# One more landing buffer for raw weight blocks, and new planner constants, in a two-layer encoder kernel

## The chip, the cores and the metric

The kernel runs on one core of one Trainium2 chip, as one program in one launch. The metric is device time in microseconds (us). Three runs of the kernel before gave 2086.12, 2087.95 and 2088.64 us; their median, 2087.95 us, is the time that the change is compared with. The profile and its trace are of one further execution of the same kernel.

## The reference

Two layers of an encoder work on 256 tokens of width 2048, all in float32. Cut to what the kernel's weight traffic is made of, a layer is:

```
h  = rms_norm(x, ln1_g);  proj = h @ w_in            # 2048 -> 4608
oa = neighborhood_attention(qa, ka, va, rpb)         # 8 heads, q and k normed with qn_a, kn_a
ob = windowed_gqa_sink(rope(qb), rope(kb), vb, sink) # 8 heads on 2, normed with qn_b, kn_b
x  = x + concat(rms_norm(oa), rms_norm(ob)) @ w_out  # 2048 -> 2048
u  = depthwise_conv(rms_norm(x, ln2_g) @ w_up)       # 2048 -> 2 x 5632, three taps and a bias
x  = x + (silu(u_gate) * u_up) @ w_down              # 5632 -> 2048
```

## The kernel before

**How a weight gets to TensorE.** All weights are read from HBM once, as half blocks of 128 x 1024 float32 (512 KB). A half block is loaded by the SP queue (`load`, L919 to L931) into a tile named `raw`, of which there are six. While the planner (below) is active, the room of the rope tables, `tabs`, serves as a seventh (L1202). TensorE multiplies in a rounded 32-bit format, so each weight is split into a high and a low part: ScalarE (ACT) copies the raw block into `whi` with rounding (`high_w`, L997), and VectorE (DVE) subtracts, `wlo = raw - whi` (`low_w_dve`, L1006). Every sixth `whi` lies in the room named `kT`. For some half blocks the low part is made by a transfer instead (`low_w`, L982 and L983): ACT writes the negated, rounded copy into `v_a` or `v_b`, and an accumulating DMA on the POOL queue adds the raw block to it. This text calls that copy the negated copy. When the last reader of a raw block is through, `free_raw` (L933) issues the next load into the same room, so a load waits, on the SP queue and in its order, until the block that was there before has been read. The activations are split in the same way (`xs`, `mid` and others hold high and low part), and three products (high x high, low x high, high x low) are summed in PSUM.

**The feed-forward half.** It takes about 630 us of each layer's 1040. An "up" quantum (two per group of 128 gate and 128 up columns) has two steps of eight matmul pairs each, a matmul of 512 columns with `whi` and one of 256 with `wlo`. `glu` then takes the result out of PSUM by two ACT copies (`read`, L646, tile `prob`), adds and scales them on DVE (L677, L649, tile `halo`), and runs the taps (L660, L662 on ACT, L687 on DVE, tile `pT`), SiLU (L689), the gating product (L666, tile `bias`) and its split (L670, L673). The down projection is done for most of the width by a scheme with seven products in place of eight: a "seven" quantum has three steps of six matmuls of 512 columns, into PSUM tiles `mm`, `tr`, `S` and `pv`. Its weight blocks come as two halves, and DVE makes sums of both halves for it: `sums_first` (L952, L953, into `prob_a`), which reads both raw halves, and `sums_second` (L958, L959, back into `raw`). Four sevens, one "plain" quantum and the "up" quanta between them make a group of some 64 us, and nine such groups follow each other in a layer. The seven holds one of two PSUM tiles named `mm`, so the "up" quantum behind it needs the other, and that one is free when both L646 copies of the "up" quantum before have run.

**What sets the order.** In this half the order on TensorE (PE), ACT, DVE and POOL is what the class `Plan` (L65 to L123) makes of a list of operations, each with an engine, a cost, a due time and dependences. `run` keeps a clock for each engine and always takes, of the operations that can begin first, the one that is due first. Due times of the weight work are set back from the step that needs it (`plan_weights`, L1014) by constants on L61: `AHEAD` for the negated copy, `HI` for `whi`, `LO` for `wlo`, `Z1` and `Z2` for the two sums. The planner keeps one clock for all transfers: L941 says that a raw half block holds it for 1.55 us and lands 2.0 us after that, L1040 says 2.9 and 2.3 us for an accumulating transfer. Each engine executes its list strictly in order, whatever the real times are. SP's order, and that of all other stages, is made by the scheduler of the language.

**Attention's room.** `add_square` (L187) sums the squares of attention's output: ACT writes a square into one of two tiles `sq` of 128 x 256, and POOL adds it to an accumulator (L191). `load_qk_g` (L297) loads the norm weights of q and k, 128 x 512, by a DMA; `rope_tables` (L311) and L314 read them on DVE. For layer 1 that load is issued when layer 0 has no more use for the room, at 231 us of the profiled execution.

Of the kernel before, what the change touches and what calls it, by code (L numbers as in the profile page):

```python
# [11 lines left out]
F32 = mybir.dt.float32  # L12
# [6 lines left out]
P = 128  # L19
L = 2  # L20
T = 256
# [3 lines left out]
HD = 128  # L25
# [32 lines left out]

EARLY = 6

AHEAD, HI, LO, Z1, Z2 = 9.0, 2.6, 1.0, 3.0, 2.0  # L61
STEP = {"up": 2.76, "seven": 1.365, "plain": 1.365, "": 1.365}


# [62 lines left out]
def encoder_kernel(  # L127
# [8 lines left out]
    act = ctx.enter_context(tc.tile_pool(name="act", bufs=1))  # L136
    work = ctx.enter_context(tc.tile_pool(name="work", bufs=2))
# [47 lines left out]
        return high  # L185

    def add_square(acc, src, first):  # L187
        sq = acc if first else work.tile([P, T], F32, name="sq", bufs=2)
        nc.scalar.activation(sq, src, AF.Square)
        if not first:  # L190
            nc.gpsimd.tensor_add(acc, acc, sq)  # L191
# [103 lines left out]
        rope["sin"], rope["cos"] = sin, cos  # L295

    def load_qk_g(l):  # L297
        par["qk_g"] = act.tile([P, 4, HD], F32, name="qk_g")
        nc.sync.dma_start(out=par["qk_g"], in_=a["qk_g"][l].partition_broadcast(P))

    def rope_tables(l):
# [330 lines left out]
    plan = Plan()  # L632
# [282 lines left out]
    raw, his, los, zs, loads, highs, homes = {}, {}, {}, {}, {}, {}, {}  # L915
# [3 lines left out]
    def load(parts=1, home="raw"):  # L919
        if loaded[0] < len(halves):  # L920
            q, h = k = halves[loaded[0]]
            loaded[0] += 1
            homes[k] = home
            if home == "raw":
                raw[k] = wp.tile([P, 1024], F32, name="raw", bufs=HALVES)
            else:
                raw[k] = act.tile([P, 1024], F32, name=home)
            m = 1024 // parts
            for j in range(parts):
                loads[q] = nc.sync.dma_start(out=raw[k][:, j * m:(j + 1) * m],  # L930
                                             in_=quanta[q][0][:, h * 1024 + j * m:h * 1024 + (j + 1) * m])  # L931

    def free_raw(k):  # L933
        del raw[k]
        home = homes.pop(k)
        if home == "raw" or plan.active:
            load(1, home)
            if plan.active and loaded[0] < len(halves):
                k2 = halves[loaded[0] - 1]
                plan.issued = max(plan.issued, plan.now, plan.done.get(("sent", *k), 0.0))  # L940
                plan.dma(("raw", *k2), plan.issued, 1.55, 2.0)  # L941

    kind_of = lambda s: quanta[steps[s][0]][2]
    is_seven = lambda s, part: s < len(steps) and kind_of(s) == "seven" and steps[s][1] == part
# [10 lines left out]
    def sums_second(q):  # L955

        z, u, w = pair(zs[q]), pair(raw[q, 0]), pair(raw[q, 1])
        nc.vector.tensor_add(u[:, 1], u[:, 1], z[:, 0])  # L958
        nc.vector.tensor_sub(u[:, 0], u[:, 1], w[:, 1])  # L959
        free_raw((q, 1))  # L960
# [7 lines left out]
    def by_transfer(s):  # L968
        q, half = steps[s]
        return half == 1 and (quanta[q][2] == "plain" or last_up.get(q, False))  # L970
# [22 lines left out]
    def high_w(s):  # L993

        if s < len(steps) and s not in his:
            his[s] = place(s, "whi")
            highs[s] = nc.scalar.activation(his[s], source(s), AF.Copy)  # L997
            if s in los:
                free_raw(steps[s])
# [14 lines left out]
    def plan_weights(s, slots):  # L1014

        q, part = steps[s]
        due = ideal[s]
        kind = kind_of(s)
        high, low = ("high_w", s), ("low_w", s)
        from_raw = [("raw", q, part)] if kind != "seven" else [("raw", q, 0)]  # L1020
        prev = [("high_w", s - 1)]
        here = lambda: (q, part if kind != "seven" else 0) in raw
        both = lambda: (q, 0) in raw and (q, 1) in raw
        slot = lambda: slots[-SPLIT_AHEAD - 1:-SPLIT_AHEAD]
        full = [("pe", *steps[s - SPLIT_AHEAD - 2])]
        if s in his and s in los:
            if not by_transfer(s):
                slots.append(("pe", q, part))
            return
        assert s not in his, s  # L1030
        if by_transfer(s):
            if s in los:
                plan.act(high, 1024, due - HI, lambda: high_w(s), prev + full, when=here)
                return
            n = turns[0] + len(sends)
            sends.append(("pe", q, part))

            def send():
                low_w(s)
                plan.dma(low, plan.now + 0.9, 2.9, 2.3)  # L1040
                plan.done["sent", q, part] = plan.done[low]

            plan.act(("negate", s), 1024, due - AHEAD, send, from_raw + sends[-3:-2] + ([("negate", negs[-1])] if negs else []), when=here)
            negs.append(s)
            plan.act(high, 1024, due - HI, lambda: high_w(s), [("negate", s)] + prev + full, when=here)
            return
        if kind == "seven" and part:
            need = [("z", q)] if part == 1 else [("z2", q)]
        else:
            need = from_raw  # L1050
        plan.act(high, 1024, due - HI, lambda: high_w(s), need + prev + full, when=here)
        plan.dve(low, 1024, due - LO, lambda: low_w_dve(s), [high] + order[-1:] + slot())
        order[:] = [low]
        slots.append(("pe", q, part))
        if kind == "seven" and part == 0:
            plan.dve(("z", q), 512, due - Z1, lambda: sums_first(q), from_raw + [("raw", q, 1)] + zlast, 2, when=both)
            zlast[:] = [("low_w", s + 1), ("z2", q)]
            plan.dve(("z2", q), 512, due - Z2, lambda: sums_second(q), [("z", q), high, low], 2)
# [59 lines left out]
    par = {}  # L1118
# [52 lines left out]
    first = {q for q in range(len(quanta)) if quanta[q][2] == "seven" and all(quanta[q - i][2] == "up" for i in range(1, 5))}  # L1171
    first = {q - 2 * (PART - 1) for q in first}
# [9 lines left out]
    def start_plan(s):  # L1182
        for e in plan.free:
            plan.free[e] = ideal[s]
        plan.active = True
        turns[1] = 0
        z = s
        while kind_of(z):
            z += 1
        for n in range(z, z + SPLIT_AHEAD):  # L1190
            assert kind_of(n) == ""
        slots = [("pe", *steps[i]) for i in range(s - SPLIT_AHEAD - 1, s) if not by_transfer(i)]
        sends[:], negs[:], order[:], zlast[:] = [], [], [], []
        for i in range(s, z + SPLIT_AHEAD):
            plan_weights(i, slots)
        for i in range(s, z):
            def body(i=i):
                q, part = steps[i]
                quanta[q][1](q, part, his.pop(i), los.pop(i))
            plan.op(("pe", *steps[i]), "PE", STEP[kind_of(i)], ideal[i], body,  # L1200
                    needs(i) + ([("pe", *steps[i - 1])] if i > s else []))
        load(1, "tabs")  # L1202

    for s, (q, half) in enumerate(steps):
        if s + SPLIT_AHEAD < KD // 2:
# [123 lines left out]
```

## Time and profile before

| | |
|---|---|
| median of three runs | 2087.95 us (2086.12 to 2088.64) |
| profiled execution, its own time | 2090.57 us |
| its span, first to last instruction | 2088.5 us |
| TensorE clock granted | 1.000 |
| busy share of the span | PE 99%, PEld 85%, DVE 82%, ACT 74%, POOL 8% |
| moved by DMA | 472.48 MB, mean 226 GB/s |

The profiled execution took 2.07 us more than its span, and 2.62 us more than the median of the runs. A row of the timeline reads: start, duration, engine, source line, operation, tiles written and read, shapes, count, and in brackets how long the engine had been idle before it and what ended that. A row of the waits reads: who waited for whom, us in total, times, longest. PE is TensorE's matmuls and PEld its weight loads; matmuls overlap, and the end of each is modelled.

### The profile page before, as it was taken

Reading aid. Unit: us, or ns where it says so; the run is one execution under the profiler, and the core shown is the slowest. Engines: PE = TensorE matmul, PEld = TensorE weight load, DVE = VectorE, ACT = ScalarE, POOL = GpSimd, SP = SyncE. Lnnn points to the kernel's source line nnn. Section 1 sums busy time; section 2 is a strip of 40 time slices with the busy share of each in tenths; the row PEclk is TensorE's granted clock in tenths of the full one; section 3 lists DMA queues with packets and bytes.
Section 4 is the critical chain, followed back from the end, with each engine's and each line's share of the span. In section 5 each row is a group of like instructions: output and inputs, shape, how many; then the busy total and the mean of one; then the engine's idle time right before and its main releaser. Section 6 shows DMA issues by size and latency. Waiting matters only on the chain.

```text
span 2088.5 us, 30567 instructions
## 1 busy us (share of the span) xinstructions
PE 2072.3 (99%) x10720; PEld 1767.6 (85%) x10720; DVE 1711.1 (82%) x2576; ACT 1548.8 (74%) x2595; POOL 157.3 (8%) x170
## 2 busy tenths in 40 slices
PE   9999999999999999999999999999999999999999
PEld 8888888888888888888888888888888888888887
DVE  7786655889999999999757766568899999999995
ACT  7566557987888888888555665579888888888883
POOL 0011100000000000000000111000000000000000
PEclk9999999999999999999999999999999999999999
DMA  9655557888888888888765555578788888888884
GB/s 347 202 164 168 166 179 213 243 236 231 259 250 247 262 248 250 246 254 256 231 182 175 171 168 167 176 214 241 239 247 242 257 256 262 248 241 259 253 250 148
DMA packets 134010, 472.48 MB, mean 226 GB/s; under 512 B 15329, under 2 KB 17889, under 8 KB 133857
## 3 DMA queue, kind: packets, MB, share of 16 engines
q1 hardware_dynamic: 117872, 413.87, 60.6%
q0 software_dynamic: 15264, 55.58, 14.3%
q8 instruction: 84, 1.38, 0.3%
q10 hardware_dynamic: 720, 1.08, 0.2%
q14 instruction: 70, 0.57, 0.1%
HBM read 412.80 MB, written 2.10 MB: 199 GB/s over the span
## 4 chain that ended last, share of the span: by engine, by line
PE 62%; DVE 18%; DMA 11%; issue 5%; ACT 4%; DVEq 0%; ACTq 0%; POOLq 0%; SPq 0%
PE mm L165 55%; DVE wlo L1006 8%; DMA raw<-in_w_up 5%; DMA raw<-in_w_seven 3%; PE S L165 2%; ACT whi L997 2%; PE pv L165 2%; DVE pT L687 1%; PE tr L165 1%; DMA tabs<-in_w_up 1%; DVE halo L649 1%; DVE prob L677 1%; DVE raw L958 1%; DVE x L800 1%; DVE x L805 1%
## 5 line engine op out<-in xcount | busy, mean ns | idle before, releaser
L165 PE MATMUL mm<-xs,whi 128*128 128x512 f32 x2320 | 813.2, 391 | 9.3 <-ACT prob L646 9.1
L1006 DVE TENSOR_TENSOR wlo<-raw,whi 128x1024 fp32r<-128x1024 f32 x535 | 651.5, 1220 | 187.1 <-ACT whi L997 161.9
L997 ACT ACTIVATE whi<-raw 128x1024 fp32r<-128x1024 f32 x613 | 640.1, 1054 | 212.6 <-PE mm L165 169.3
L165 PE MATMUL mm<-xs,wlo 128*128 128x256 f32 x2112 | 597.1, 283 | 0.0
L165 PEld LDWEIGHTS mm<-xs,whi 128*128 128x128 f32 x2320 | 435.2, 188 | 109.7 <-ACT prob L646 19.3
L165 PEld LDWEIGHTS mm<-xs,wlo 128*128 128x128 f32 x2112 | 398.9, 189 | 4.5 <-DVE wlo L1006 0.4
L165 PE MATMUL mm<-whi,xs 128*128 128x512 f32 x1152 | 294.8, 393 | 0.2 <-ACT whi L997 0.2
L165 PE MATMUL mm<-whi,mid 128*128 128x512 f32 x928 | 255.4, 393 | 0.4 <-ACT v_a L330 0.4
L165 PEld LDWEIGHTS mm<-whi,xs 128*128 128x128 f32 x1152 | 212.9, 188 | 42.8 <-ACT whi L997 0.6
L165 PEld LDWEIGHTS mm<-whi,mid 128*128 128x128 f32 x928 | 169.9, 188 | 34.1 <-ACT v_a L330 0.9
L165 PE MATMUL mm<-xs,kT 128*128 128x512 f32 x496 | 174.6, 390 | 0.0
L165 PE MATMUL mm<-wlo,xs 128*128 128x512 f32 x576 | 158.9, 392 | 0.0
L662 ACT ACTIVATE pT<-halo,conv 128x256 f32<-128x256 f32 x352 | 157.7, 496 | 0.0
L165 PE MATMUL mm<-wlo,mid 128*128 128x512 f32 x486 | 152.5, 393 | 0.0
L687 DVE TENSOR_TENSOR pT<-pT 128x512 f32<-128x512 f32 x176 | 121.0, 687 | 12.3 <-ACT pT L660 4.1
L165 PEld LDWEIGHTS mm<-wlo,xs 128*128 128x128 f32 x576 | 107.1, 188 | 21.4
L646 ACT ACTIVATE prob<-mm 128x512 f32<-128x512 f32 x176 | 102.4, 584 | 30.5 <-PE mm L165 29.5
L165 PEld LDWEIGHTS mm<-xs,kT 128*128 128x128 f32 x496 | 93.1, 188 | 19.5
L165 PEld LDWEIGHTS mm<-wlo,mid 128*128 128x128 f32 x486 | 90.9, 188 | 19.2
L660 ACT ACTIVATE pT<-halo,conv 128x256 f32<-128x256 f32 x176 | 103.4, 589 | 0.0
L165 PE MATMUL mm<-xs,v_a 128*128 128x256 f32 x352 | 99.3, 282 | 0.0
L165 PE MATMUL mm<-xs,v_b 128*128 128x256 f32 x352 | 99.3, 282 | 0.0
(233 smaller groups left out, 2958.4 us busy)
## 6 DMA issues: line engine op xcount, KB each, us to landing
raw<-in_w_up SPq DMA_DIRECT2D x302, 512.0 KB, 5.2
raw<-in_w_in SPq DMA_DIRECT2D x142, 512.0 KB, 4.4
raw<-in_w_seven SPq DMA_DIRECT2D x126, 512.0 KB, 5.3
raw<-in_w_out SPq DMA_DIRECT2D x64, 512.0 KB, 3.8
tabs<-in_w_up SPq DMA_DIRECT2D x50, 512.0 KB, 5.1
v_a<-raw POOLq DMA_DIRECT2D x46, 512.0 KB, 6.4
v_b<-raw POOLq DMA_DIRECT2D x46, 512.0 KB, 6.5
raw<-in_w_plain SPq DMA_DIRECT2D x32, 512.0 KB, 5.7
```

What stands on the lines that cost most here:

```text
L165: nc.tensor.matmul(ps, lhsT, rhs, start=start, stop=stop, skip_group_check=True)
L646: nc.scalar.activation(own[part], ps[:, :, part], AF.Copy)
L649: nc.vector.tensor_mul(ux[:, :, r:r + T], own[0], st["r2"][:, None, :].to_broadcast([P, 2, T]))
L660: nc.scalar.activation(own["y"][:, j], src, AF.Identity, scale=taps[j][i], bias=taps[j][3])
L662: nc.scalar.activation(own[name][:, j], src, AF.Copy, scale=taps[j][i])
L677: plan.dve(k("sum"), 512, e + 5.0, lambda: nc.vector.tensor_add(own[0], own[0], own[1]), [k("t"), k("t2")])
L687: lambda n=n: nc.vector.tensor_add(own["y"], own["y"], own[n]),
L800: plan.dve(k("x_2"), 1024, e + 13.4, lambda: add(x_2, x_2, both(ps[5])), [("pe", q, 2), k("x12b")])
L805: plan.dve(k("x2_"), 1024, e + 22.0, lambda: add(x2_, x2_, both(cur["t"])), [k("t7"), k("x_2"), k("x21")])
L958: nc.vector.tensor_add(u[:, 1], u[:, 1], z[:, 0])
L997: highs[s] = nc.scalar.activation(his[s], source(s), AF.Copy)
L1006: nc.vector.tensor_sub(los[s], source(s), his[s].bitcast(F32))
```

## The change

The change has two parts.

**Room.** The squares and the norm weights, until now two tiles of 128 x 256 and one of 128 x 512, become parts of one tile `aux` of 128 x 1024: `add_square` alternates between its third and fourth quarter, and the norm weights are its first half. While the planner is active, `aux` takes one more raw half block, as `tabs` does (`load(1, "aux")` in `start_plan`). So eight half blocks have room where seven had.

**Constants.** The planner's due times move ahead (`AHEAD` 9.0 to 10.5, `HI` 2.6 to 3.2, `LO` 1.0 to 1.4, `Z1` 3.0 to 4.2, `Z2` 2.0 to 3.5), and its transfers take longer: a raw half block 1.65 us on the transfer clock (was 1.55) and 3.2 us from there to its landing (was 2.0), an accumulating one 3.2 us to its landing (was 2.3).

```
-AHEAD, HI, LO, Z1, Z2 = 9.0, 2.6, 1.0, 3.0, 2.0
+AHEAD, HI, LO, Z1, Z2, TAKES, LANDS = 10.5, 3.2, 1.4, 4.2, 3.5, 1.65, 3.2
...
     def add_square(acc, src, first):
-        sq = acc if first else work.tile([P, T], F32, name="sq", bufs=2)
+        if first:
+            sq = acc
+        else:
+            par["square"] ^= 1
+            sq = par["aux"][:, 512 + T * par["square"]:512 + T * par["square"] + T]
...
     def load_qk_g(l):
-        par["qk_g"] = act.tile([P, 4, HD], F32, name="qk_g")
+        par["aux"], par["square"] = act.tile([P, 1024], F32, name="aux"), 0
+        par["qk_g"] = par["aux"][:, 0:4 * HD].rearrange("p (w d) -> p w d", w=4)
...
-                plan.dma(("raw", *k2), plan.issued, 1.55, 2.0)
+                plan.dma(("raw", *k2), plan.issued, TAKES, LANDS)
...
-                plan.dma(low, plan.now + 0.9, 2.9, 2.3)
+                plan.dma(low, plan.now + 0.9, 2.9, LANDS)
...
         load(1, "tabs")
+        load(1, "aux")
```

After the change the kernel's lines stand four lines lower from L192 on, and five from L300 on: L997 is L1002, L1006 is L1011, L982 is L987, L930 is L935, L646 is L651, L952 is L957.

**The loads on SP** in layer 0, for the "up" step whose negated copy ACT begins at 497.36 us of the profiled execution, two blocks ahead of it and the two around it. The names in brackets are what a load waits for: DVE, ACT or the landing of an earlier DMA (DMAHW an ordinary one, DMASW an accumulating one). Before, with that step's block going into `raw_4859`:

```order
L930 DMA raw_4816<-in_w_up 128x1024 [waits DMAHW0_49,DVE_49]
L930 DMA raw_4842<-in_w_up 128x1024 [waits DMAHW2_49,DVE_49]
L930 DMA tabs_4848<-in_w_up 128x1024 [waits DMAHW5_49,DMASW5_49,Activation_49]
L930 DMA raw_4859<-in_w_up 128x1024 [waits DMAHW3_49,DVE_49]
L930 DMA raw_4890<-in_w_seven 128x1024 [waits DMAHW4_49,DVE_49]
```

Now the same five blocks, the step's block going into `tabs_4836`:

```order
L935 DMA raw_4773<-in_w_up 128x1024 [waits DMAHW7_49,DMAHW0_49,DVE_49]
L935 DMA raw_4804<-in_w_up 128x1024 [waits DVE_49]
L935 DMA raw_4830<-in_w_up 128x1024 [waits DMAHW1_49,DVE_49]
L935 DMA tabs_4836<-in_w_up 128x1024 [waits DMAHW2_49,DMAHW4_49,DMASW5_49,Activation_49]
L935 DMA raw_4847<-in_w_seven 128x1024 [waits DMAHW3_49,DVE_49]
```

Each block now waits for the release that the block ahead of it waited for: the wait for ACT and an accumulating DMA stood at the third load and stands at the fourth, with that step's block.

**ACT** around the same negated copy (`v_a`), down to the two copies out of PSUM (`prob<-mm`) that TensorE needs. Before:

```order
L997 ACTIVATE whi<-prob_a 128x1024
L982 ACTIVATE v_a<-raw 128x1024
L689 ACTIVATE prob<-pT 128x256
L997 ACTIVATE whi<-raw 128x1024
L670 ACTIVATE mid<-bias 128x256
L997 ACTIVATE whi<-raw 128x1024 x2
L646 ACTIVATE prob<-mm 128x512
L997 ACTIVATE kT<-tabs 128x1024
L646 ACTIVATE prob<-mm 128x512
```

Now:

```order
L1002 ACTIVATE whi<-prob_a 128x1024
L694 ACTIVATE prob<-pT 128x256
L987 ACTIVATE v_a<-tabs 128x1024
L675 ACTIVATE mid<-bias 128x256
L1002 ACTIVATE whi<-raw 128x1024 x3
L651 ACTIVATE prob<-mm 128x512
L1002 ACTIVATE kT<-raw 128x1024
L651 ACTIVATE prob<-mm 128x512
```

SiLU (`prob<-pT`) moves ahead of the negated copy; the other copies keep their places but for one. In most later groups SiLU moves back instead, at 28 places in all: at half of them behind one `whi` copy, at the others behind the negated copy and one `whi` copy.

**DVE** a few us later at the same place, where the two sums of a seven's halves (`prob_a`) stand with the subtractions (`wlo`) and the sum of the "up" results (`prob<-prob`). Before:

```order
L1006 TENSOR_TENSOR wlo<-raw,whi 128x1024
L677 TENSOR_TENSOR prob<-prob 128x512
L1006 TENSOR_TENSOR wlo<-tabs,kT 128x1024
L649 TENSOR_TENSOR halo_115<-prob,acc_b 128x2x256
L952 TENSOR_TENSOR prob_a<-raw 128x512
L953 TENSOR_TENSOR prob_a<-raw 128x512
```

Now:

```order
L1011 TENSOR_TENSOR wlo<-raw,whi 128x1024
L957 TENSOR_TENSOR prob_a<-raw,aux 128x512
L958 TENSOR_TENSOR prob_a<-aux,raw 128x512
L682 TENSOR_TENSOR prob<-prob 128x512
L1011 TENSOR_TENSOR wlo<-raw,whi 128x1024
L654 TENSOR_TENSOR halo_115<-prob,acc_b 128x2x256
```

The two sums, which read both halves of a seven's block, have moved ahead of the addition and of one subtraction.

Two moves outside the planner: the first raw block that goes into `aux` is loaded during the output projection, behind attention's last square; and layer 1's norm weights are no longer loaded at 231 us but at the end of layer 0's feed-forward half, when the last weight block in `aux` has been split. There the first L316 of layer 1 stands on DVE right behind the subtraction that reads that last block, and waits for the load of the norm weights.

## The prediction

> **What bounds the kernel now.** I read the page first, then TensorE's waits, then the places where it waits.
>
> ```profile
> span 2088.5 us, 30567 instructions
> ## 1 busy us (share of the span) xinstructions
> PE 2072.3 (99%) x10720; PEld 1767.6 (85%) x10720; DVE 1711.1 (82%) x2576; ACT 1548.8 (74%) x2595; POOL 157.3 (8%) x170
> ```
>
> TensorE is busy for 99% of the span, and the change takes no matmul away. What can go is idle time. TensorE's waits say for whom:
>
> ```profile
> PE mm L165 <- ACT prob L646: 9.1, 17, 0.9
> ...
> PE pv L165 <- DVE wlo L1006: 0.8, 3, 0.3
> ...
> PE S L165 <- DVE wlo L1006: 0.2, 1, 0.2
> ```
>
> 17 waits are for the copy out of PSUM (L646), four for a low part. Idle time is less than what a wait costs, because the end of a matmul is modelled past the moment at which the next could start. The chain of waits gives the pace without waits, the timeline the start on either side of a wait:
>
> ```profile
> 420.66 1.36 PE S L165 x6
> ```
>
> ```profile
> 502.57 0.39 PE L165 MATMUL mm<-wlo,mid 128*128 128x512 f32 x1
> 503.84 0.50 PE L165 MATMUL mm<-xs,whi 128*128 128x512 f32 x1 [0.88 <-ACT prob L646]
> ```
>
> Six matmuls of 512 columns take 1.36 us, 0.227 each, while one is shown as 0.39. The one at 503.84 could have started at 502.57 + 0.23 = 502.80, so 1.04 us were lost, 0.88 shown and 0.16 hidden. The 17 waits cost 9.1 + 17 x 0.16 = 11.8 us, the four for low parts 1.0 + 4 x 0.16 = 1.6 us: together 13.4 us, 0.64% of the span. This is all that the change can win.
>
> Why ACT is late with L646 stands in its timeline:
>
> ```profile
> 497.36 1.06 ACT L982 ACTIVATE v_a<-raw 128x1024 fp32r<-128x1024 f32 x1 [2.73 <-DMA raw<-in_w_up]
> 498.32 0.40 ACT L689 ACTIVATE prob<-pT 128x256 f32<-128x256 f32 x1
> 498.63 1.05 ACT L997 ACTIVATE whi<-raw 128x1024 fp32r<-128x1024 f32 x1
> 499.58 0.40 ACT L670 ACTIVATE mid<-bias 128x256 fp32r<-128x256 f32 x1
> 499.89 2.00 ACT L997 ACTIVATE whi<-raw 128x1024 fp32r<-128x1024 f32 x2
> 501.79 0.57 ACT L646 ACTIVATE prob<-mm 128x512 f32<-128x512 f32 x1
> 502.26 1.05 ACT L997 ACTIVATE kT<-tabs 128x1024 fp32r<-128x1024 f32 x1
> 503.21 0.58 ACT L646 ACTIVATE prob<-mm 128x512 f32<-128x512 f32 x1
> ```
>
> ACT stood 2.73 us before the negated copy, because its raw block had not landed. Behind that it runs without a gap up to the second L646, which ends at 503.79; TensorE starts at 503.84. So of the 2.73 us of waiting 1.04 reach TensorE: the slack here is 1.69 us. These waits recur:
>
> ```profile
> ACT v_a L982 <- DMA raw<-in_w_up: 32.3, 18, 4.9
> ...
> ACT v_b L982 <- DMA raw<-in_w_up: 28.9, 16, 4.1
> ```
>
> 34 waits, 61.2 us, 1.8 us on average. The planner believed that the block would be there.
>
> **The change part by part.**
>
> *The eighth room.* The rows of the order show that every load gets the release that the load ahead of it had. What that does to the landing is read from the block and the one ahead of it:
>
> ```profile
> 489.39 0.33 SPq L930 DMA_DIRECT2D tabs<-in_w_up  x1
> 489.82 0.38 SPq L930 DMA_DIRECT2D raw<-in_w_up  x1
> ```
>
> ```profile
> tabs<-in_w_up SPq DMA_DIRECT2D x1, 512.0 KB, 6.6
> raw<-in_w_up SPq DMA_DIRECT2D x1, 512.0 KB, 7.5
> ```
>
> The block ahead landed at 489.39 + 6.6 = 496.0, this one at 489.82 + 7.5 = 497.3. If issues move up by one place in an unchanged stream of transfers, this block lands when the one ahead did, 1.3 us earlier. ACT's wait falls to 2.73 - 1.3 = 1.4 us, below the slack of 1.69: the 1.04 us are gone. I check the place with the longest wait of layer 1 that I found:
>
> ```profile
> 1859.37 1.06 ACT L982 ACTIVATE v_a<-raw 128x1024 fp32r<-128x1024 f32 x1 [2.85 <-DMA raw<-in_w_up]
> ```
>
> ```profile
> 1864.76 0.39 PE L165 MATMUL mm<-wlo,mid 128*128 128x512 f32 x1
> 1865.86 0.50 PE L165 MATMUL mm<-xs,whi 128*128 128x512 f32 x1 [0.70 <-ACT prob L646]
> ```
>
> ```profile
> 1851.24 0.33 SPq L930 DMA_DIRECT2D raw<-in_w_up  x1
> 1852.06 0.33 SPq L930 DMA_DIRECT2D raw<-in_w_up  x1
> ```
>
> ```profile
> 1852.06 7.23 DMA raw<-in_w_up
> ```
>
> ```profile
> raw<-in_w_up SPq DMA_DIRECT2D x1, 512.0 KB, 6.8
> ```
>
> The loss is 1865.86 - 1864.99 = 0.87 us, the slack 2.85 - 0.87 = 1.98. The block landed at 1859.29; the one ahead, whose row of the DMA view is the last, 6.8 us after 1851.24, at 1858.0. 1.3 us earlier leaves a wait of 1.6, again under the slack. The longest of the 17 idle times is 0.9, a loss of 1.04, and 1.3 is more than that. Taken at full, the eighth room wins the 11.8 us. I keep 0.9 of it, 10.6 us, for places where a second delay stands close behind the first.
>
> *Is there transfer time for it?* The windows around the place:
>
> ```profile
> 480.00:485.00 5.00, 5.00 (x28) 4.27 (x27) 4.96 (x8) 3.85 (x4) 0.86 (x1) 1.00 0.50 129
> 485.00:490.00 5.00, 4.71 (x23) 3.37 (x22) 5.00 (x8) 3.98 (x6) 0.00 (x0) 1.00 1.04 287
> 699.00:763.00 64.00, 63.66 (x341) 54.72 (x340) 60.22 (x86) 53.57 (x89) 4.36 (x5) 1.00 0.85 254
> ```
>
> The last two columns are the DMA engines' share and GB/s. Half of the five us before the burst is idle, 2.5 us; a half block at the 287 GB/s of the burst takes 524 KB / 287 = 1.8 us and fits.
>
> On how long such a block takes, a rule of the Trainium skill stands against this change. "DMA: Bandwidth & Descriptors", section "Anatomy of one DMA", fits a transfer from the POOL queue as 2.0 us plus its bytes over 436 GB/s; that makes an estimate of 3.2 us for 512 KB. By it the block of 489.82 would land at 493.0, ACT would never wait, and the eighth room would win nothing. The row shows 7.5 us, so the trace disagrees: blocks queue behind each other here.
>
> *The constants.* On ACT the same copies stand between the negated copy and the second L646; only SiLU (0.40 us) changes sides. Where it moves ahead, slack grows by 0.3; where it moves back, L646 sees the same instructions before it. Moving SiLU back, at 28 places of the order, delays the gating product on DVE by one or two copies of 0.95 us (499.58 - 498.63). What covers it is that the seven that reads the product comes only some steps later, by the planner's due times a dozen us. I cost it at nothing; without that cover it would be up to 28 x 1.4 = 40 us of DVE's waiting, which reaches TensorE only through late `wlo`. The larger `LO`, `Z1` and `Z2` put weight work earlier on DVE, which is what the four waits for low parts lack; I take half of their 1.6 us, 0.8.
>
> *The room's other users.* Squares alternate between two quarters as between two tiles: nothing. The norm weights of layer 1 add a wait on DVE at the layers' boundary: the first L316 waits for a landing, and behind it queue an addition to x and the next subtractions. The nearest rows:
>
> ```profile
> 1017.92 1.23 DVE L1006 TENSOR_TENSOR wlo<-raw,whi 128x1024 fp32r<-128x1024 f32 x1 [0.48 <-ACT whi L997]
> 1023.22 1.23 DVE L1006 TENSOR_TENSOR wlo<-raw,whi 128x1024 fp32r<-128x1024 f32 x1 [4.08 <-PE mm L165]
> ```
>
> ```profile
> bias<-in_bias SPq DMA_DIRECT2D x1, 160.0 KB, 3.8
> ```
>
> The subtraction that frees `aux` is the one at 1017.92 and ends at 1019.15. A small load then lands 3.8 us later, at 1023.0, inside the 4.08 us that DVE waits for TensorE anyway. So nothing is lost. If the landing takes the 7.5 us of a busy stretch instead, DVE is 3.5 us late, and at worst TensorE too; below nothing it can't go, as no wait ends there.
>
> *The sum*, against the profiled execution: span 2088.5 - 10.6 - 0.8 = 2077.1, its own time 2090.57 - 11.4 = 2079.2. That execution was 2.6 us above the median of the runs. From the median, 2087.95 - 11.4 = 2076.5 us.
>
> **The rivals.**
>
> *A landing follows its issue* (0.14). If each block keeps its 7.5 us from issue to landing, only the issue's 0.43 us (489.82 - 489.39) count: 0.43 of 1.04, 41% of 11.8 = 4.9 us, 2083.0 us. For it: the small load at the boundary landed after 3.8 us, these after 6.6 and 7.5; what stretches a landing in a busy stretch may stretch it whenever it was issued. Against it: 6.6 and 7.5 us for two blocks issued 0.43 us apart, a queue and not a fixed time.
>
> *The bound moves to DVE or nothing moves* (0.09). DVE is busy 60.2 of 64 us in a group. If it takes over each stall as ACT's lateness goes, or SP's loads are held by something that I don't see, the time stays within 4 us of 2088. Against it: without the losses (11.8 us over 18 groups, 0.7 each) a group takes 63.3 us, and DVE still has 3.1.
>
> *Slower: the sums wait in front of the others* (0.05).
>
> ```profile
> DVE prob_a L952 <- DMA raw<-in_w_seven: 23.6, 25, 2.5
> ```
>
> DVE already waits 25 times for a seven's second half. `Z1` puts the sums 1.2 us earlier, ahead of the addition and a subtraction, which now queue behind that wait, and L649 and TensorE behind these. At full, 25 x 1.2 = 30 us of new DVE waiting. If half reaches TensorE, 15 - 11.4 makes 2091.6 us. It decides from 11.4 of 30, 38%. Against it: these blocks too land 1.3 us earlier, which cancels the 1.2, and 3.1 us per group are spare.
>
> **How the numbers follow.** The forecast, losses nearly gone, has 0.72: 2076.5 us, between 2073 (13.4 us and a little more, 2087.95 - 13.4 = 2074.6, less a spread of about 1.3 between runs) and 2080 (the norm weights' 3.5 us lost). A landing that follows its issue reaches to 2083. The range 2073 to 2083 holds these two, 0.86. A measurement here can tell about 0.2%, 4.2 us, from no change. Faster by more than that, below 2083.8: 0.72 + 0.14 and a little of the third case, 0.87. Within it 0.09, slower 0.04.
>
> **What would show it.** In the profile after: PE's waits for the L651 copy fall from 17 and 9.1 us to a few and under 2; ACT's waits of the negated copy for DMA fall from 61 us to under 30, by about 1.3 us each; the load at this place is issued at the former one's moment and lands 1.3 us earlier against TensorE's steps; DVE waits under 4 us at the first L316 of layer 1 with no wait of TensorE behind it. I am wrong if ACT's waits shrink and TensorE's don't (something else is close behind), if landings keep 7.5 us from their issue, or if PE's waits for low parts (`wlo`) grow.

## The result, and the profile after

The kernel after takes 2070.26 us (median of 6 runs, 2069.91 to 2070.64), the kernel before 2088.3 us on the same chip (6 runs, 2086.12 to 2091.91): a ratio of 0.9911, 95% interval 0.9898 to 0.9924, 18.0 us less. The forecast was 2076.5 us, with a range from 2073 to 2083: the direction was right, and the gain larger than the range allowed, and larger than the 13.4 us that the prediction called all that could be won. The profiled execution after took 2070.64 us, with this span and busy time:

```profile
span 2068.9 us, 30510 instructions
...
PE 2062.4 (100%) x10720; PEld 1769.9 (86%) x10720; DVE 1706.1 (82%) x2576; ACT 1549.3 (75%) x2595; POOL 157.6 (8%) x170
```

The span is 19.6 us shorter. All of it is in the feed-forward halves, counted here from the first transposes of `x` (L216 before), which begin inside the output projection, so that they are longer than the stretch that the planner orders: layer 0's lasts 727.6 us where it lasted 737.5, layer 1's 735.4 where it lasted 745.2, and attention of layer 1 with both boundaries 302.9 us in both kernels.

TensorE's waits after, in us in total, times, longest:

```profile
PE pv L165 <- DVE halfpi L161: 1.1, 1, 1.1
PE mm L165 <- ACT whi L179: 0.7, 1, 0.7
PE mm L165 <- ACT v_a L335: 0.4, 2, 0.2
```

The 17 waits for the copy out of PSUM and the four for a low part in the feed-forward halves are gone from these rows; what is left stands in attention and at the start. At the place that the prediction worked out, SP's queue now shows the load of the step whose negated copy goes to `v_a`:

```profile
485.80 0.33 SPq L935 DMA_DIRECT2D tabs<-in_w_up  x1
```

ACT after it:

```profile
493.00 1.07 ACT L987 ACTIVATE v_a<-tabs 128x1024 fp32r<-128x1024 f32 x1 [0.30 <-DMA tabs<-in_w_up]
...
497.99 0.59 ACT L651 ACTIVATE prob<-mm 128x512 f32<-128x512 f32 x1
498.48 1.05 ACT L1002 ACTIVATE kT<-raw 128x1024 fp32r<-128x1024 f32 x1
499.43 0.59 ACT L651 ACTIVATE prob<-mm 128x512 f32<-128x512 f32 x1
```

And TensorE at the matmul that waits for the second of these two copies out of PSUM (before, the one at 503.84):

```profile
501.65 0.40 PE L165 MATMUL mm<-wlo,mid 128*128 128x512 f32 x1
501.88 0.39 PE L165 MATMUL mm<-xs,whi 128*128 128x512 f32 x1
502.12 0.28 PE L165 MATMUL mm<-xs,wlo 128*128 128x256 f32 x1
```

ACT's wait for the block is 0.30 us where it was 2.73, the second copy ends at 500.02, and TensorE's matmul comes 0.23 us after the one ahead of it, without a wait. The load is issued 501.88 - 485.80 = 16.1 us ahead of this matmul; before it was 502.80 - 489.82 = 13.0 us ahead of the moment at which the matmul could have run. So it is issued 3.1 us earlier against TensorE's work, not 0.43. It still takes 7.1 us to land.

A group of the feed-forward half, whose window took 64.00 us before:

```profile
697.00:760.30 63.30, 63.30 (x341) 54.90 (x340) 60.22 (x86) 54.25 (x89) 4.37 (x5) 1.00 0.85 255
```

It takes 63.30 us, with TensorE (the first number behind the window's length) busy in all of it and DVE (the third) for the same 60.22 us as before: DVE had those 3.1 us to spare and has not become the bound.

### The profile page after: what moved, and what is told of

It is laid out like the page before. It is cut to its first block, busy times and chain, and to the rows that moved or that the text cites. A ratio compares the mean times of both kernels' runs of the same rounds, so it can differ in the third digit from the quotient of the medians.

```text
span 2068.9 us, 30510 instructions
## 1 busy us (share of the span) xinstructions
PE 2062.4 (100%) x10720; PEld 1769.9 (86%) x10720; DVE 1706.1 (82%) x2576; ACT 1549.3 (75%) x2595; POOL 157.6 (8%) x170
## 3 DMA queue, kind: packets, MB, share of 16 engines
q1 hardware_dynamic: 117872, 413.87, 61.2%
## 4 chain that ended last, share of the span: by engine, by line
PE 99%; DMA 0%; ACT 0%; ACTq 0%; DVE 0%; issue 0%
PE mm L165 85%; PE S L165 6%; PE pv L165 4%; PE tr L165 3%; PE tr L460 1%; PE tr L381 1%; PE S L220 1%; DMA mid<-in_xT 0%; ACT v_a L335 0%; ACT whi L1002 0%; ACT mid L182 0%; ACT xs L182 0%; DVE x L872 0%; ACTq L1105 0%; ACTq L1098 0%
## 5 line engine op out<-in xcount | busy, mean ns | idle before, releaser
L1011 DVE TENSOR_TENSOR wlo<-raw,whi 128x1024 fp32r<-128x1024 f32 x503 | 613.0, 1220 | 185.0 <-ACT whi L1002 162.4
L1002 ACT ACTIVATE whi<-raw 128x1024 fp32r<-128x1024 f32 x569 | 596.2, 1055 | 222.2 <-PE mm L165 182.8
L667 ACT ACTIVATE pT<-halo,conv 128x256 f32<-128x256 f32 x352 | 157.8, 498 | 0.0
L651 ACT ACTIVATE prob<-mm 128x512 f32<-128x512 f32 x176 | 103.6, 591 | 50.2 <-PE mm L165 49.8
L665 ACT ACTIVATE pT<-halo,conv 128x256 f32<-128x256 f32 x176 | 103.7, 590 | 0.0
```

Source lines behind the costliest of these rows:

```text
L651: nc.scalar.activation(own[part], ps[:, :, part], AF.Copy)
L665: nc.scalar.activation(own["y"][:, j], src, AF.Identity, scale=taps[j][i], bias=taps[j][3])
L667: nc.scalar.activation(own[name][:, j], src, AF.Copy, scale=taps[j][i])
L1011: nc.vector.tensor_sub(los[s], source(s), his[s].bitcast(F32))
```

## A measure that closes the account

TensorE's rows of waits do not add up to 19.6 us, since they count only what is left after the modelled end of the matmul before. The weight loads (PEld) end sooner, so the same waits show more of themselves there. Before:

```profile
PEld mm L165 <- ACT prob L646: 19.3, 25, 1.3
PEld pv L165 <- DVE wlo L1006: 3.4, 7, 0.8
PEld S L165 <- DVE wlo L1006: 1.1, 3, 0.6
```

25 waits for the copy, not 17, and ten of the two kinds of waits for low parts that the prediction counted as four. One that the matmul's rows do not show at all stands at 552.49 (before, timeline of TensorE's two queues):

```profile
552.14 0.40 PE L165 MATMUL mm<-wlo,qtok 128*128 128x512 f32 x1
552.49 0.19 PEld L165 LDWEIGHTS mm<-xs,whi 128*128 128x128 f32 x1 [0.39 <-ACT prob L646]
552.49 0.50 PE L165 MATMUL mm<-xs,whi 128*128 128x512 f32 x1
552.79 0.19 PEld L165 LDWEIGHTS mm<-xs,wlo 128*128 128x128 f32 x1
552.82 0.36 PE L165 MATMUL mm<-xs,wlo 128*128 128x256 f32 x1
```

The matmul starts 0.35 us after the one ahead of it, 0.12 more than the 0.23 of the pace, and its row has no bracket. The next one starts 0.33 us later, another 0.10: its weights could not be loaded ahead. The same restart stands behind the long wait at 503.84:

```profile
503.84 0.50 PE L165 MATMUL mm<-xs,whi 128*128 128x512 f32 x1 [0.88 <-ACT prob L646]
504.18 0.28 PE L165 MATMUL mm<-xs,wlo 128*128 128x256 f32 x1
504.30 0.39 PE L165 MATMUL mm<-xs,whi 128*128 128x512 f32 x1
504.53 0.28 PE L165 MATMUL mm<-xs,wlo 128*128 128x256 f32 x1
```

0.34 us from the first to the second, and then 0.12 for 256 columns and 0.23 for 512.

So I count **late starts**: for each two consecutive matmuls of the two feed-forward halves, the time between their starts less the pace of the first (0.227 us for 512 columns, 0.118 for 256), where more than 0.06 us is left. Before this gives 98 late starts, 21.9 us: 26 of over 0.18 us, 14.6 us; 33 small ones right behind another late one, 3.5 us; 39 other small ones, 3.8 us. After it gives 27, 2.6 us. The difference, 19.3 us, is the span's 19.6. Of it 14.2 us are stalls, 3.4 us restarts behind them, and 1.7 us delays too small for a row.

The second measure, **lead**, puts each load, landing and negated copy on a clock that counts only TensorE's work (the paces of the matmuls begun by then), and compares it with the same load or copy of before: a mean over 444 loads and 84 copies inside the two feed-forward halves. After, landings come 3.4 us earlier than before, and negated copies 1.7 us earlier.

All kernels by these measures but e4, which is told below. The runs with e1 to e3, with e5 to e8 and with e9 to e12 were made on three other chips than the first, so kernels of different groups are best compared by their ratios. Rooms is the number of half blocks that have room; told is what the planner believes of landings; due the five due times. The ratio is to the kernel before on the same chip, with its 95% interval. The last column is what ACT waited for landings at the negated copies.

| kernel | rooms | told | due | us | ratio | span | late starts, us | landings earlier | copies earlier | ACT's waits |
|---|---|---|---|---|---|---|---|---|---|---|
| before | 7 | old | old | 2088.3 | | 2088.5 | 21.9 | 0 | 0 | 69.8 in 40 |
| room alone (e1) | 8 | old | old | 2086.80 | 0.9985 [0.9974, 0.9996] | 2083.6 | 16.8 | 2.3 | 1.6 | 70.1 in 42 |
| constants alone (e2) | 7 | new | new | 2080.36 | 0.9959 [0.9946, 0.9973] | 2077.4 | 10.4 | -1.0 | -1.2 | 18.9 in 10 |
| six rooms (e3) | 6 | old | old | 2109.22 | 1.0090 [1.0068, 1.0112] | 2107.2 | 40.9 | -3.1 | -2.7 | 92.0 in 68 |
| e5 | 8 | new | old | 2070.83 | 0.9918 [0.9903, 0.9934] | 2069.0 | 2.9 | 3.5 | 1.7 | 38.2 in 30 |
| e6 | 8 | old | new | 2081.44 | 0.9966 [0.9956, 0.9977] | 2082.0 | 14.2 | 2.3 | 1.5 | 58.0 in 37 |
| e7 | 7 | new | old | 2104.02 | 1.0076 [1.0060, 1.0092] | 2101.8 | 35.0 | -1.9 | -2.0 | 59.8 in 34 |
| e8 | 7 | old | new | 2081.96 | 0.9969 [0.9955, 0.9983] | 2082.4 | 16.1 | 0.3 | 0.3 | 75.6 in 44 |
| lead untold (e9) | 8 | see below | old | 2070.83 | 0.9904 [0.9889, 0.9918] | 2069.2 | 2.9 | 3.2 | 1.4 | 46.2 in 31 |
| e10 | 8 | 4.4 us | old | 2070.50 | 0.9902 [0.9886, 0.9919] | 2068.4 | 2.2 | 1.8 | -1.1 | 16.4 in 6 |
| e11 | 7 | raw new | old | 2118.69 | 1.0132 [1.0115, 1.0149] | 2116.0 | 49.3 | -1.7 | -1.7 | 67.2 in 38 |
| e12 | 7 | new | DVE's new | 2087.90 | 0.9990 [0.9975, 1.0004] | 2087.1 | 20.7 | -1.0 | -1.1 | 49.5 in 32 |
| after | 8 | new | new | 2070.26 | 0.9911 [0.9898, 0.9924] | 2068.9 | 2.6 | 3.4 | 1.7 | 41.7 in 27 |

In every row but e6 the span's difference from before is that of the late starts to within 0.5 us (e7: 13.3 and 13.1; e11: 27.5 and 27.4); in e6 it is 6.5 against 7.7, and why is open. TensorE's late starts are the time. ACT's waits are not: e7 has 59.8 us of them and is slower than before, e9 has 46.2 and is as fast as e10 with 16.4.

## The experiments

**Which part wins: the room alone, the constants alone, one room less, and waits put in.** Room alone, against the kernel after:

```
-AHEAD, HI, LO, Z1, Z2, TAKES, LANDS = 10.5, 3.2, 1.4, 4.2, 3.5, 1.65, 3.2
+AHEAD, HI, LO, Z1, Z2, TAKES, LANDS = 9.0, 2.6, 1.0, 3.0, 2.0, 1.55, 2.0
...
-                plan.dma(low, plan.now + 0.9, 2.9, LANDS)
+                plan.dma(low, plan.now + 0.9, 2.9, 2.3)
```

> The room without the constants: the changed kernel with eight rooms for raw half blocks, and all constants as before (AHEAD 9.0, HI 2.6, LO 1.0, Z1 3.0, Z2 2.0, 1.55 and 2.0 us for a raw block, 2.3 for an accumulating transfer). If the room is what wins (earlier issue, earlier landing), the time is 2070 to 2074 us and ACT's waits of the negated copy for a landing, 69.9 us before and 41.7 after, are near 42. If the planner's truer picture of landings is what wins, the time is 2083 to 2088 us and those waits stay near 70.

2086.80 us. The room, by itself, wins 2 or 3 us. The waits that the prediction spoke of are gone, and others have taken their place; TensorE's weight loads:

```profile
PEld mm L165 <- ACT kTb L789: 12.7, 11, 1.9
PEld mm L165 <- DVE wlo L1011: 3.9, 10, 0.7
...
PEld mm L165 <- ACT prob L651: 0.7, 2, 0.5
```

`kTb` (L789) is ACT's copy of one half of a seven's PSUM tile `mm`, made nine times a layer; the third step of the same seven writes the tile's other half, and TensorE's first matmul of it waits for the copy. Why it is late stands, at one of these places, on ACT some 13 us ahead of it:

```profile
907.96 1.06 ACT L987 ACTIVATE v_a<-raw 128x1024 fp32r<-128x1024 f32 x1 [2.10 <-DMA raw<-in_w_plain]
...
920.52 0.59 ACT L789 ACTIVATE kTb<-mm 128x512 f32<-128x512 f32 x1
```

TensorE then:

```profile
921.16 0.74 PE L165 MATMUL mm<-whi,mid 128*128 128x512 f32 x2 [1.42 <-ACT kTb L789]
```

In the kernel after, the same negated copy stands behind the taps (L665, L667) instead of ahead of them, 7.9 us ahead of `kTb` and not 12.6, and does not wait:

```profile
903.37 1.05 ACT L987 ACTIVATE v_a<-raw 128x1024 fp32r<-128x1024 f32 x1
...
911.23 0.59 ACT L789 ACTIVATE kTb<-mm 128x512 f32<-128x512 f32 x1
```

The delay comes down by way of DVE. In e1 DVE waits 1.67 us, up to 910.00, for the `whi` copy that stands behind the negated copy, then runs with hardly a gap up to L716, for which ACT waits 1.09 us at 918.77; from there ACT's list leads straight to `kTb`.

ACT's waits for blocks of a plain quantum are new in this kernel, 35.5 us in all:

```profile
ACT v_b L987 <- DMA raw<-in_w_plain: 17.8, 8, 2.6
ACT v_a L987 <- DMA raw<-in_w_plain: 17.7, 8, 3.0
```

The planner, told that blocks are loaded earlier and land 2.0 us after their transfer, moves their copies forward as well: landings come 2.3 us earlier and copies 1.6 us earlier, and ACT waits 70.1 us (65.5 of them, 37 times, for blocks in `raw`) where it waited 69.8. This is the second of the two cases that were expected.

The constants alone: the kernel after without the line `load(1, "aux")`.

> The constants without the room: the changed kernel with seven rooms while the planner is active (aux holds squares and norm weights only), and all new constants. If the room is what wins, 2084 to 2090 us, with TensorE still waiting some 17 times for the copy out of PSUM. If the planner's constants win, 2070 to 2075 us and those waits are gone. If the two only win together, both this kernel and the one with the room alone stay above 2080 us.

2080.36 us, 8 or 9 us won with seven rooms. Landings come 1.0 us later here, not earlier, and copies 1.2 us later: by planning with later landings ACT stops waiting for them (18.9 us in 10), and TensorE still waits for L651 ten times, 7.3 us on its weight loads. Room and constants alone win some 3 and 9 us; together 18.

One room less: the kernel before without the line `load(1, "tabs")`.

> One room fewer than before: the kernel before without tabs as seventh room. If the depth of loads sets ACT's lateness, the slack of 1.4 to 2.0 us behind each negated copy is used up already, so a landing that comes 1.3 to 3 us later reaches TensorE in full, in 18 groups and twice in most: 20 to 60 us more, 2108 to 2150 us, all of it as TensorE's waits in the feed-forward halves. If depth is not what matters (a landing follows the drain of the queue), 2086 to 2092 us.

2109.22 us, 19 us slower. Loads are issued 3.2 us later against TensorE's work and land 3.1 us later. 444 loads go into some 1080 us of TensorE's work, one every 2.4 us; that is what one place in the queue is worth on average, and the rest is that releases are later themselves.

Waits put in: the kernel after, with the second L651 copy made seven times over in six quanta of each layer. The repeated copies write the same values; only ACT comes late with them.

```
-                nc.scalar.activation(own[part], ps[:, :, part], AF.Copy)
+                for _ in range(7 if part and f % 5 == 0 and 10 <= f < 40 else 1):
+                    nc.scalar.activation(own[part], ps[:, :, part], AF.Copy)
```

> The price of one wait of TensorE: the changed kernel with the second copy out of PSUM done seven times over in 12 chosen places (six per layer), which makes TensorE wait there by up to 2 us each and changes no value. By the prediction's price, span minus 2068.9 us equals the idle time that TensorE's waits show plus 0.16 us for each of them. If a wait also costs a restart of 0.11 us (the second matmul behind a wait comes 0.34 us after the first, not 0.23, since its weight load was not ahead), it equals the idle time plus 0.27 us for each, and waits of TensorE's weight loads are more than those of its matmuls. Expected: 12 waits, 0.3 to 2 us each, 2073 to 2090 us in span.

One run, 2105.63 us, span 2103.9: 35.0 us more than after, and 37.5 - 2.6 = 34.9 us more of late starts. TensorE's rows show 16.5 us in 8 waits for this copy and 2.4 us in eight for low parts that after does not have; with 0.27 us for what each hides and restarts (0.16 and 0.11, sixteen times) that makes 23 us, not 35. So the expectation missed: the waits were longer than 2 us, the span lies above 2090, and neither price per wait closes the account. Most of the rest is something that the kernel before never ran into, and it is told at the end; some 4 us stay open.

**Which constants: the other four of the eight combinations.** Rooms, told landings and due times make eight kernels; before, after, e1 and e2 are four of them. e5 and e7 have `AHEAD` to `Z2` as before and `TAKES, LANDS` new; e6 and e8 the reverse, with 2.3 us for accumulating transfers; e7 and e8 are without `load(1, "aux")`. My theory P was that the told landings are what the room needs; the rival D said the due times.

> Eight rooms with the new landings and the old due times. Theory P (the room's lead is spent by the planner unless it knows the later landings: with the room alone ACT still waited 65.5 us in 37 negated copies, and TensorE 11 times for the copy of the seven, kTb): with the landings put right ACT's waits fall to about 42 us, TensorE's waits for prob and kTb vanish and the time is 2071 us, within 2 of the whole change. Rival D (it is the due times that keep ACT's copies for TensorE in time, the landings hardly matter): about 2086 us, as with the room alone, with kTb waits still there. Third: the two share the work, 2078 us.

> Eight rooms with the new due times and the old landings. Theory P: the planner still puts the negated copies where the block has not landed, ACT waits 60 us or more there, and the time is about 2085 us. Rival D: 2071 us, ACT's waits about 42 us and no kTb waits. Third (both share): 2078 us.

> Seven rooms with the new landings and the old due times. Theory P: the landings are what the two kinds of constants won together with seven rooms, so about 2080.5 us with ACT's waits near the 19 us of that kernel. Rival D: 2088 us, nothing won. Third: 2084 us.

> Seven rooms with the new due times and the old landings. Theory P: nothing won, about 2088 us, with ACT's waits for DMA still near 70 us; the time may even rise a little, since copies that are due earlier meet blocks that have landed even less. Rival D: about 2080.5 us. Third: 2084 us.

With eight rooms theory P holds for the greater part. e5, 2070.83 us, has everything that the whole change has. e6, 2081.44, lies between the 2085 of P and the 2078 of a shared effect, so with eight rooms the due times add some 4 us to what the room wins; it keeps the wait for `kTb`:

```profile
PE mm L165 <- ACT kTb L789: 5.0, 7, 1.3
```

With seven rooms it falls. Later landings by themselves make the kernel slower (e7, 2104.02 us), and the due times by themselves make it faster (e8, 2081.96). The waits of e7:

```profile
PEld mm L165 <- DVE wlo L1011: 12.9, 16, 2.6
PEld mm L165 <- ACT prob L651: 8.9, 14, 1.8
PEld pv L165 <- DVE wlo L1011: 6.9, 9, 1.0
```

**The room without the planner's knowing.** If e1 is slow because the planner spends the lead, then eight rooms with the planner's list left as it was must be fast. Against e1, the planner books at each release the landing of the block ahead of the one that is loaded, so its clock and its lists for PE, ACT, DVE and POOL in the feed-forward halves stay those of seven rooms, and only the loads come one place earlier. This is the prediction's premise, issues up by one place in an unchanged order, by itself:

```
+            if plan.active and loaded[0] < len(halves):
+                untold.append(halves[loaded[0]])
+                plan.done[("raw", *untold[-1])] = 1e9
             load(1, home)
-            if plan.active and loaded[0] < len(halves):
-                k2 = halves[loaded[0] - 1]
+            if plan.active and untold and untold[0] != halves[-1]:
+                k2 = untold.pop(0)
...
```

> Eight rooms with all old constants, and the planner is not told of the lead: at each release it books the landing of the block ahead of the one that is loaded, so it makes the order of the seven rooms, word for word that of before on ACT and DVE in the two feed-forward halves, while each load is issued one place earlier. Theory P (the room alone wins little only because the planner, told of earlier blocks, moves the negated copies forward as well: landings 2.3 us earlier against TensorE's work, copies 1.6 us earlier): here landings come some 2.4 us earlier and the copies do not, the longest wait of 2.85 us goes below its slack of 1.98, TensorE's waits for prob vanish and the time is 2072 us, between 2070 and 2076. Rival O (the order of seven rooms is itself too tight, and other waits, for kTb or low parts, come up as in the kernel with the room alone): 2080 to 2087 us.

2070.83 us, all old constants, nothing new but the load's place: the whole gain. In the trace ACT, DVE, POOL and TensorE run the same instructions in the same order as in the kernel before, in the stretches that the planner orders. Its weight loads' waits:

```profile
PEld mm L165 <- ACT prob L651: 1.0, 2, 0.5
```

Landings come 3.2 us earlier and the copies, in the same order, 1.4 us, as ACT is less late with them. The rival, that the order of seven rooms is too tight, is out.

**Later still, and why seven rooms lose.**

> Eight rooms, old due times, landings told 1.2 us later still (4.4 us, also for the accumulating transfers). Theory C (a circle: a later landing on the planner's clock puts the reading of blocks later, so rooms come free later and loads are issued later; a room is worth 2.4 us of it, so eight rooms can stand 3.2 and seven cannot): 4.4 costs the circle another turn, landings come 1 to 2 us later than with 3.2 and the time rises to between 2076 and 2095 us. Rival L (later is safer as long as there are eight rooms): 2070 to 2072 us, ACT's waits for landings under 20 us.

2070.50 us with `LANDS` at 4.4: theory C, the circle, falls, and the rival L holds, ACT's waits included (16.4 us in 6). With eight rooms the two late settings that were run, 3.2 and 4.4 us, are as good as each other.

e11 is e7 with 2.3 us again for accumulating transfers; e12 is e7 with `LO`, `Z1` and `Z2` new.

> Seven rooms, old due times, and only the raw blocks told to land later (1.65 and 3.2 us), the accumulating transfers as before (2.3 us). Seven rooms with both told later took 2104 us. Theory C, in which what hurts is that the planner reads and frees later: the accumulating transfers hold rooms too, so without their 0.9 us about half of the 15.5 us of loss stays, 2093 to 2099 us. Rival A (all of the loss is from the accumulating transfers, whose believed landing holds back the planner's later loads): about 2088 us. Rival B (all of it is from the raw blocks): 2104 us.

> Seven rooms, new landings, and of the due times only those of DVE's work (LO, Z1, Z2) new, those of ACT's copies (AHEAD, HI) old. With all due times old this took 2104 us, with all new 2080 us. With all old, TensorE waited most for wlo from DVE (20.9 us in 29 on its weight loads) and DVE 25.4 us for the second half of a seven. Theory D (the sums of the sevens are taken too late, and their earlier due times heal it): 2080 to 2086 us. Rival H (the copies of ACT heal it): 2098 to 2104 us.

e11 took 2118.69 us, worse than any of the three said: telling the accumulating transfers late as well had not hurt, it had helped. e12 took 2087.90 us, a little outside theory D's range and far from H's: DVE's due times win back 16 to 18 of the 24 us between e7 and e2 (by the times and by the ratios), which is theory D for the greater part. In e11 TensorE waits for low parts from DVE most of all:

```profile
PEld mm L165 <- DVE wlo L1011: 19.3, 18, 3.2
```

and in e12 far less than in e11 or e7:

```profile
PEld mm L165 <- DVE wlo L1011: 5.3, 5, 2.8
```

So with seven rooms the largest part of the loss stands on DVE, and earlier due times there mend most of it; which of `LO`, `Z1` and `Z2` does so was not separated. It is not all of the loss: in e11 TensorE's weight loads also wait 16.6 us, 16 times, for low parts made by a transfer; the kernel before has no such row. Why the planner puts them late there when it is told of later landings was not settled; none of my theories on it held in all three runs.

## Why the prediction was right in direction and too small

*That ACT's lateness, from landings, makes TensorE wait, and that issues moved up by one place end it:* right. e9 does that alone and wins all.

*"This is all that the change can win", 13.4 us:* this step failed, and with it the forecast's 11.4 us, which were taken from it. It counted 21 waits from TensorE's matmul rows. The late starts were 98 and 21.9 us. The stalls among them were close to the prediction's term, 14.6 us in 26 against 13.4 in 21; the restarts behind them, 3.5 us, and the delays under 0.18 us, 3.8 us, have no row among the matmul's waits, and were not in it. The weight loads' rows, 25 waits and ten, would have shown the missing ones.

*The factor of 0.9, and half of the low parts' waits:* not needed. No second delay stood close behind: 14.2 of 14.6 us of stalls went. From the 11.4 us of the forecast to 19.3 us of late starts it is 2.8 us here and in the waits not counted, 3.4 in restarts, and 1.7 in small delays.

*"This block lands when the one ahead did, 1.3 us earlier":* right in direction and too small; at that place it is 3.5 us (landing to matmul 501.88 - 492.9 = 9.0 us, before 502.80 - 497.3 = 5.5), and 3.4 us on average. The prediction took the distance of two landings in a burst. The mean distance of loads, 2.4 us, is nearer; what comes on top fits with each earlier copy freeing its own room earlier for the next load, but that share was not measured by itself. By the prediction's own reasoning 1.3 us was enough, since it lay above the longest loss, 1.06 us; whether it would have been is not shown, as no run with the order unchanged has so small a lead.

*Transfer time:* it was there. With one more block in flight landings take 5.6 us in the median after and 5.2 before (`raw<-in_w_up`), against 3.4 us of lead. The rule of the Trainium skill that spoke against the change ("DMA: Bandwidth & Descriptors", "Anatomy of one DMA") is fitted for transfers from the POOL queue; taken for these loads on SP, as the prediction took it, it would have let the room win nothing. e9 won 19.7 us with the room alone, so the measurement decides against it here.

*The constants, costed at nothing:* right for the change as a whole, since after and e9 differ by 0.6 us (on two chips), and wrong as a picture of the parts. The prediction read the order of after, in which the constants had already undone what the room does to the planner. Without them the planner spends the lead, and 15 of the 18 us are gone (e1). The 0.8 us from `LO`, `Z1` and `Z2` are not seen: e5, without them, is as fast within 0.6 us.

*The norm weights:* as worked out. DVE waits 3.80 us at the first L316 of layer 1, below the 4 that the prediction named, and no wait of TensorE follows; the boundary's 302.9 us are unchanged.

*The rivals.* A landing that follows its issue: half right in its premise, since the block still takes 7.1 us from its issue, and wrong in the size of the issue's move, 3.1 us and not 0.43. DVE as the bound: no, 60.22 of 63.30 us. Sums in front of the others: DVE's waits of the first sum for a seven's second half, 23.6 us in 25 before, are fewer after:

```profile
DVE prob_a L957 <- DMA raw<-in_w_seven: 4.5, 3, 2.6
```

*What should have shown it:* ACT's waits fell from 61.2 us (blocks of the up projection in `raw`) to 30.6, and with the other rooms from 69.8 to 41.7, a little above the bound of 30 that the prediction set. What remains of them costs next to nothing: e9 with 46.2 us of them and e10 with 16.4 are equally fast.

## What to carry to other kernels

A planner that writes fixed lists for in-order engines from assumed landing times turns any lead it is told of into an earlier order: a new buffer may win little until its lead is kept from the planner or the assumed landings are put on the late side, so test the buffer with the order unchanged. What a tuned, TensorE-bound kernel like this can still win is the sum of late matmul starts, weight-load waits and restarts included, not the idle time that TensorE's rows show. One place in the queue of loads moved landings by 3.1 to 3.4 us here (e3 and after), somewhat more than the mean distance of loads, 2.4 us, and far more than the 1.3 us between two landings in a burst.

## What the runs showed of the hardware

**A wait of two microseconds can cost half the clock for three more.** In e4, TensorE at one of the waits put in:

```profile
718.48 0.39 PE L165 MATMUL mm<-wlo,mid 128*128 128x512 f32 x1
720.68 0.68 PE L165 MATMUL mm<-xs,whi 128*128 128x512 f32 x1 [1.81 <-ACT prob L652]
721.16 0.41 PE L165 MATMUL mm<-xs,wlo 128*128 128x256 f32 x1
```

The same kernel's windows of one us, with the granted clock third from the end:

```profile
720.00:721.00 1.00, 0.32 (x1) 0.32 (x2) 0.34 (x1) 0.97 (x3) 0.00 (x0) 0.92 0.25 102
721.00:722.00 1.00, 1.00 (x4) 0.81 (x4) 1.00 (x2) 1.00 (x2) 0.00 (x0) 0.50 0.02 8
...
724.00:725.00 1.00, 1.00 (x6) 0.88 (x6) 0.93 (x3) 1.00 (x4) 0.00 (x0) 0.87 0.82 303
725.00:726.00 1.00, 1.00 (x7) 0.89 (x6) 1.00 (x2) 1.00 (x3) 0.00 (x0) 1.00 0.89 336
```

A share of 0.92 in a window means that the clock was at half for twice the missing 0.08. So it is at half from about 720.84 (0.08 x 2 us ahead of 721) to 724.26 (0.13 x 2 us behind 724), 3.4 us. Of e4's eight late starts between 2.0 and 3.9 us, five were followed by such a stretch, and each lost about 1.6 us more (1.76 us of late starts in the next 78 matmuls, against 0.18 behind the others). 5 x 1.6 = 8 us make up most of what the waits of e4 leave open. The kernel before, whose longest late start is 1.06 us, had none, and of the late starts above 2.0 us three of four had one in the kernel with six rooms, neither of two in e7, two of four in e11 and both in e12: the length of the wait alone does not decide it.

Where it lies does, as far as these traces go. Within each run all changes of the granted clock lie a whole multiple of 3.413 us apart (in e4 the half-clock stretches begin at 557.00, 638.92, 720.84, 888.10 and 1686.82 us). Cut a run's time into such steps: in all twelve cases, of four runs, the step ahead of the slow stretch holds at least 1.98 us of one late start. Seven late starts of 2.0 to 3.1 us that a step's end splits, with no more than 1.8 us in either step, had no slow stretch behind them (e4's at 1605.57 and 1933.01 among them). One case does not fit: e4's 1.98 us at 1768.67, which end 0.06 us ahead of a step's end. The Trainium skill ("TensorE: Matmul & The Clock Gate", "HAM oscillation — how this bites in real kernels") warns of idle gaps above about 3.4 us; here late starts of 2.0 us, 1.8 of them shown as idle, were enough, while the length of the slow stretch agrees with the window that the page gives.

**A matmul's wait costs more than its row.** Beyond the idle time shown, 0.16 us hide under the modelled end of the matmul before, and about 0.11 us go at the second matmul behind the wait, whose weights were not loaded ahead.
